# A layer step on one core: the sample tokens' part of a depthwise convolution moved from VectorE to GpSimd

## The chip, the cores and the metric

The kernel runs on one core of a Trainium2 chip. Its time is the device time of one execution in microseconds; a kernel is judged by the median of several executions. The profile shows one execution: TensorE (PE, with its weight loads as PEld), VectorE (DVE), ScalarE (ACT), GpSimd (POOL), and the queues from which SyncE (SP), ACT and POOL issue DMAs. Every engine and every queue works through its own instructions in one fixed order.

## The reference, cut to what matters

One layer of a gated decoder is computed for 1024 prompt tokens and 64 sample tokens (8 sequences of 8) at width 1024. A combined input projection gives a convolution value and gate, q, k and v of three attention groups, and several gates. The attention branch runs dilated windows; the convolution branch is

```python
u = a_val * jax.nn.sigmoid(a_gate)                     # (tokens, 1024 channels)
# prompt: 30 zeros in front; sample: the last 30 values of each sequence in front (state_conv)
u_hist = jnp.concatenate([state_conv, u], axis=1)
conv_raw = depthwise_valid(u_hist, conv_w)             # out[t, c] = sum_j conv_w[j, c] * u_hist[t + j, c], j = 0..30
c = jax.nn.silu(layer_norm(conv_raw + conv_b, conv_ln_g, conv_ln_b))
```

Both branches are gated, projected, merged, projected again and normalised. All arithmetic is in float32. The updated caches are outputs too.

## The kernel before

The 1088 tokens (1024 prompt, then 64 sample) lie along the free axis, channels on the 128 partitions. Every projection tile (128 output channels) is three chunks of 384, 352 and 352 tokens, and each chunk is 24 matmuls: 8 blocks of the inner width, each as three products of a high and a low part (`proj_chunk`, L186). For that ACT makes a high part of each weight tile (`split`, L117) and DVE the low part (L118). Two buffers each hold the raw, high and low weight tiles; the raw tile's load (L130) is on SP's queue.

The order of every engine's instructions is fixed when the program is built: a planner simulates the engines and takes, for each, the instruction that is ready and has the highest priority. `tc.high_priority(LP)` with LP = -800 puts the convolution's arithmetic behind everything else that is ready.

The stages: the loads and the first projections, with V projected for the three groups (to 318 us in the profile); the prompt's attention in 12 units (4 head pairs by 3 groups), between which the q and k projections of the unit two ahead and the convolution's channel tiles 0 to 4 are placed (`B_CONV`); the sample's attention in four pairs `pr` with convolution tiles 5 to 7 (`W_CONV`) and the merge gates; then the LayerNorm over the convolution's channels (reading the results back from a DRAM buffer `cvd`, L771), and the output projections, which are on TensorE alone in the main.

In the prompt's attention a burst of scores S goes through PE (L346), DVE (bias and minimum, L356), ACT (exponent, L363), PE (transposes, L375), DVE and ACT (copies, L383 and L381) and PE (values, L399). `combine` weighs three groups, and its small transfers (L446 `stn`, L473 `wd`, L478 `wb`) and the statistics' stores (L426, L430 `scr`) are issued from POOL. In the sample's attention, POOL copies the queries into a spread-out tile `qf` (L646, 24 copies for a pair) that PE's score matmuls (L655, L663, L667) read.

For channel tile c, `conv_inputs` projects gate and value and leaves u in two tiles: `ub` (30 zeros and 1024 prompt values; two buffers, slots 21 and 22) and `us` (8 sequences of 30 state and 8 new values, 304 columns; three views that lie in the `keep` tiles). The state's columns come by a DMA from SP (L493); the new ones are written last by DVE (L514). POOL stores the convolution states (L515, L516). `conv` then runs 31 taps on DVE, each as one instruction over the prompt's 1024 columns (L526, L529) and one over the 64 sample values (L527, L531), into one tile `cv` (slot 23), which POOL stores into `cvd` (L533). The sample's taps 0 to 22 read state columns alone, so that they can run ahead of the projection; taps 23 to 30 need u.

Of the kernel before, what the change touches and what calls it, by code (L numbers as in the profile page):

```python
# [11 lines left out]
ALU = mybir.AluOpType  # L12
# [4 lines left out]
P = 128  # L17
D = 1024
KT = D // P
NP_ = 1024  # L20
NS = 64
NT = NP_ + NS
# [19 lines left out]
def trunk_kernel(ctx, tc, I, O):  # L42
    nc = tc.nc
    sync, act, dve, pool, pe = nc.sync, nc.scalar, nc.vector, nc.gpsimd, nc.tensor
# [12 lines left out]
    def nm(s):  # L57
        uid[0] += 1
        return f"{s}_{uid[0]}"

    def slot(i, shape, dt=F32, n="s"):
        return sp.tile(shape, dt, tag=f"S{i}", name=nm(n))
# [39 lines left out]
    for q in range(4):  # L102
        w = slice(q * 256, (q + 1) * 256)
# [3 lines left out]
    for q in range(2):  # L107
        w = slice(q * 512, (q + 1) * 512)
# [13 lines left out]
    def cload(name, shape):  # L122
        t = const.tile(shape, F32, name=nm(name))
        sync.dma_start(out=t, in_=I[name])
        return t

    def load_w(src, n, raw=None, parts=1):
        if raw is None:
            raw = wp.tile([P, D], F32, tag="raw", name=nm("raw"))
            sync.dma_start(out=raw[:, :n], in_=src)  # L130
        hi = wp.tile([P, D], F32R, tag="hi", name=nm("hi"))
        lo = wp.tile([P, D], F32R, tag="lo", name=nm("lo"))
        with tc.high_priority(HP):
            for i in range(0, n, n // parts):
                s = split(hi[:, i:i + n // parts], lo[:, i:i + n // parts], raw[:, i:i + n // parts])
            pace(s)
        return hi, lo
# [29 lines left out]
    convw = cload("conv_w", [P, 8, 31])  # L167
    convb = cload("conv_b", [P, 8])
# [47 lines left out]
    keep = [slot(18, [P, NT], n="keep"), None, slot(20, [P, NT], n="keep")]  # L216
# [3 lines left out]
    usv = []  # L220
# [266 lines left out]
    cvd = dram.tile([8, P, NT], F32, name="cvd")  # L487

    def conv_inputs(c):
        ub = slot(21 + c % 2, [P, PAD + NP_], n="ub")  # L490
        us = usv[c % 3]
        pool.memset(ub[:, :PAD], 0.0)
        sync.dma_start(out=us[:, :, :PAD], in_=I["state_conv"][c])  # L493
        wg = load_w(I["w_in"][F_AGATE + c], D)
        wv = load_w(I["w_in"][F_AVAL + c], D)
        b = b_sb[:, F_AVAL + c:F_AVAL + c + 1]
        bg = b_sb[:, F_AGATE + c:F_AGATE + c + 1]

        def spans(c0, cn):

            n = min(cn, NP_ - c0)
            out = [(slice(0, n), ub[:, PAD + c0:PAD + c0 + n], lambda a: a)]
            if n < cn:
                out.append((slice(n, cn), us[:, :, PAD:], lambda a: a.rearrange("p (b t) -> p b t", b=8)))
            return out

        for c0, cn in CHUNKS:
            ps = proj_chunk([(*wg, xhi, xlo)], c0, cn)
            for sl, dst, view in spans(c0, cn):
                act.activation(out=dst, in_=view(ps[:, sl]), func=AF.Sigmoid, bias=bg)  # L510
        for c0, cn in CHUNKS:
            ps = proj_chunk([(*wv, xhi, xlo)], c0, cn)
            for sl, dst, view in spans(c0, cn):
                dve.scalar_tensor_tensor(out=dst, in0=view(ps[:, sl]), scalar=b, in1=dst, op0=ALU.add, op1=ALU.mult)  # L514
        pool.dma_start(out=O["convp"][c], in_=ub[:, NP_:])  # L515
        pool.dma_start(out=O["convs"][c], in_=us[:, :, 8:])  # L516
        return ub, us

    def conv(c, ub, us):
        acc = slot(23, [P, NT], n="cv")  # L520
        accs = acc[:, NP_:].rearrange("p (b t) -> p b t", b=8)
        for j in range(31):
            w = convw[:, c, j:j + 1]
            if j == 0:
                cb = convb[:, c:c + 1]
                dve.tensor_scalar(out=acc[:, :NP_], in0=ub[:, :NP_], scalar1=w, scalar2=cb, op0=ALU.mult, op1=ALU.add)  # L526
                dve.tensor_scalar(out=accs, in0=us[:, :, :8], scalar1=w, scalar2=cb, op0=ALU.mult, op1=ALU.add)  # L527
            else:
                dve.scalar_tensor_tensor(out=acc[:, :NP_], in0=ub[:, j:j + NP_], scalar=w, in1=acc[:, :NP_],  # L529
                                         op0=ALU.mult, op1=ALU.add)  # L530
                dve.scalar_tensor_tensor(out=accs, in0=us[:, :, j:j + 8], scalar=w, in1=accs,  # L531
                                         op0=ALU.mult, op1=ALU.add)
        pool.dma_start(out=cvd[c], in_=acc)  # L533


    snew = dram.tile([3, 8, NS, NS], F32, name="snew")
# [43 lines left out]
    for u, (f, g) in enumerate(units):  # L580
        if g == 0:
            res = []
        q, k = qk.pop(u)
        sample_new_scores(f, g, q, k)
        scr = None if g == 0 else dram.tile([NP_, 4], F32, name=nm("scr"))
        res.append(prompt_attention(f, g, q, k, load_v(f, g), scr))
        if g == 0 and todo:
            combine(*todo.pop())
        if u + 2 < len(units):
            project_qk(u + 2)  # L590
        if u < 2:
            project_v(u + 1)
            if u == 1:
                keep[1] = slot(19, [P, NT], n="keep")
                usv += [keep[i][:, c:c + 304].rearrange("p (b t) -> p b t", b=8)
                        for i, c in ((0, 12 * NS), (1, 0), (1, 304))]
        if u in B_CONV:
            c = B_CONV.index(u)
            cu = conv_inputs(c)
            with tc.high_priority(LP):  # L600
                conv(c, *cu)
        if g == 2:
            attn[f] = slot(14 + f, [P, NT], n="attn")
            todo.append((f, res))
# [143 lines left out]
    def gate(f, dst):  # L748
        pool.dma_start(out=dst, in_=gated(f, AF.Sigmoid, rotate("gst", (3, 4))))
# [3 lines left out]
    for pr in range(4):  # L753
        sc = sample_scores(pr)
        if pr == 0:
            combine(*todo.pop())
            kvs += [9, 10, 11]
            odt += [slot(12 + i, [P, 2, 512], n="od") for i in range(2)]
        for c in W_CONV[pr]:
            u = conv_inputs(c)  # L760
            with tc.high_priority(LP):
                conv(c, *u)
        sample_values(pr, *sc)
        for _ in range(4):
            gate(*gates.pop(0))
    sample_out()
    credit[1] = 1.25
    cv = []
    for c in range(8):
        t = slot(6 + c, [P, NT], n="cv")  # L770
# [76 lines left out]
    for i in range(8):  # L847
        hi, lo = load_w(I["w_b"][i], 512)
        t = slot((0, 1, 2, 3, 16, 17, 4, 5)[i], [P, NT], n="tf")
# [40 lines left out]
    for i, t in enumerate((0, 1, 2, 3, 8, 4, 5, 6, 7)):  # L890
        n = min(P, NT - t * P)
# [14 lines left out]
        for c0, cn in ((0, 512), (512, 256), (768, 256)) if last else ((0, 512), (512, 512)):  # L906
# [8 lines left out]
            for j, (a, b) in enumerate(ops):  # L915
                pe.matmul(ps[:, :cn], a, b, start=(j == 0), stop=(j == len(ops) - 1))  # L916
            dve.scalar_tensor_tensor(out=r[:n, s], in0=xr[:n, s], scalar=ALPHA, in1=ps[:n, :cn],
                                     op0=ALU.mult, op1=ALU.add)
# [12 lines left out]
        for s in parts:  # L931
            dve.scalar_tensor_tensor(out=y[:n, s], in0=r[:n, s], scalar=mv[:n, 0:1], in1=lng[:n, s],
                                     op0=ALU.subtract, op1=ALU.mult)
        dve.reciprocal(out=mv[:n, 4:5], in_=mv[:n, 3:4])
        newton(mv[:n, 4:5], mv[:n, 2:3], mv[:n, 5:6])
        for s in parts:
            dve.scalar_tensor_tensor(out=y[:n, s], in0=y[:n, s], scalar=mv[:n, 4:5], in1=lnb[:n, s],
                                     op0=ALU.mult, op1=ALU.add)
# [136 lines left out]
```

## Time and profile before

| what | value |
|---|---|
| median of 3 runs | 1416.22 us (1413.43, 1416.22, 1421.27) |
| profiled execution, its own time | 1413.38 us |
| its span, first to last instruction | 1411.6 us |
| mean granted TensorE clock | 0.999 |
| busy: PE / PEld / DVE / ACT / POOL | 1394.8 / 1265.8 / 844.0 / 444.7 / 162.9 us |

Busy time is the time in which at least one instruction of an engine is under way. Instructions of PE and of DVE overlap a little with the next one, so that durations are longer than the distance between starts.

### The profile page before, as it was taken

Reading aid. Unit: us, or ns where it says so; the run is one execution under the profiler, and the core shown is the slowest. Engines: PE = TensorE matmul, PEld = TensorE weight load, DVE = VectorE, ACT = ScalarE, POOL = GpSimd, SP = SyncE. Lnnn points to the kernel's source line nnn. Section 1 sums busy time; section 2 is a strip of 40 time slices with the busy share of each in tenths; the row PEclk is TensorE's granted clock in tenths of the full one; section 3 lists DMA queues with packets and bytes.
Section 4 is the critical chain, followed back from the end, with each engine's and each line's share of the span. In section 5 each row is a group of like instructions: output and inputs, shape, how many; then the busy total and the mean of one; then the engine's idle time right before and its main releaser. Section 6 shows DMA issues by size and latency. Waiting matters only on the chain.

```text
span 1411.6 us, 21936 instructions
## 1 busy us (share of the span) xinstructions
PE 1394.8 (99%) x8682; PEld 1265.8 (90%) x8682; DVE 844.0 (60%) x1632; ACT 444.7 (32%) x984; POOL 162.9 (12%) x302
## 2 busy tenths in 40 slices
PE   9999999999999999999999999999999999999997
PEld 8989888899999998999887788898899999999886
DVE  4223131328959779599989785681367425335686
ACT  5204041134434434246531212122246422103220
POOL 2010111110111111102270402000000000000000
PEclk9999999999999999999999999999999999999999
DMA  6629385265855575656488666549653437435321
GB/s 232 215 102 337 117 299 208 87 225 173 249 180 186 197 217 160 219 173 180 138 245 332 244 259 263 165 184 373 223 191 134 162 111 230 142 93 157 120 90 75
DMA packets 85110, 271.27 MB, mean 192 GB/s; under 512 B 20912, under 2 KB 40688, under 8 KB 83600
## 3 DMA queue, kind: packets, MB, share of 16 engines
q1 hardware_dynamic: 70704, 147.16, 31.0%
q10 hardware_dynamic: 2816, 87.30, 17.6%
q0 software_dynamic: 11488, 35.42, 7.6%
q8 instruction: 68, 1.11, 0.3%
q14 instruction: 34, 0.28, 0.1%
HBM read 236.39 MB, written 120.74 MB: 253 GB/s over the span
## 4 chain that ended last, share of the span: by engine, by line
PE 83%; DVE 8%; DMA 3%; issue 3%; ACT 2%; POOL 1%; SPq 0%; DVEq 0%; ACTq 0%; POOLq 0%
PE mm L186 57%; PE mm L284 9%; PE mm L916 7%; DVE cv L529 4%; PE S L346 2%; PE O L399 1%; PE PT L375 1%; ACT P L363 1%; PE O L700 1%; PE S L655 1%; DMA wb<-wd 1%; PE mm L292 1%; DVE lo L118 1%; DVE P L356 1%; PE S L663 1%
## 5 line engine op out<-in xcount | busy, mean ns | idle before, releaser
L186 PE MATMUL mm<-x,hi 128*128 128x352 f32 (+1 forms) x3648 | 912.8, 330 | 1.0 <-ACT x L117 0.6
L186 PEld LDWEIGHTS mm<-x,hi 128*128 128x128 f32 x3648 | 643.3, 188 | 35.0 <-issue 28.9
L186 PE MATMUL mm<-x,lo 128*128 128x352 f32 (+1 forms) x1824 | 600.2, 329 | 0.0
L186 PEld LDWEIGHTS mm<-x,lo 128*128 128x128 f32 x1824 | 342.5, 188 | 12.3 <-issue 10.8
L529 DVE SCALAR_TENSOR_TENSOR cv<-ub,conv_w,cv 128x1024 f32<-128x1024 f32 x240 | 307.1, 1280 | 1.9
L117 ACT ACTIVATE hi<-raw 128x1024 fp32r<-128x1024 f32 (+2 forms) x88 | 86.1, 980 | 272.0 <-PE mm L186 214.2
L118 DVE TENSOR_TENSOR lo<-raw,hi 128x1024 fp32r<-128x1024 f32 (+2 forms) x88 | 98.9, 1125 | 103.5 <-ACT hi L117 91.6
L284 PE MATMUL mm<-vhi,x 128*128 128x512 f32 x384 | 119.1, 390 | 0.0
L363 ACT ACTIVATE P<-P,st 128x128 f32<-128x128 f32 (+1 forms) x192 | 84.2, 440 | 74.7 <-DVE st L356 69.3
L744 ACT ACTIVATE gst<-mm,b_in 128x352 f32<-128x352 f32 (+1 forms) x72 | 40.1, 558 | 150.0 <-PE mm L186 113.8
L284 PEld LDWEIGHTS mm<-vhi,x 128*128 128x128 f32 x384 | 72.1, 188 | 15.0 <-issue 0.2
L285 DVE TENSOR_TENSOR vst<-mm,vb 128x512 f32<-128x512 f32 x24 | 16.6, 692 | 104.8 <-PE mm L284 104.8
L284 PE MATMUL mm<-vlo,x 128*128 128x512 f32 x192 | 74.9, 390 | 0.0
L531 DVE SCALAR_TENSOR_TENSOR cv<-keep,conv_w,cv 128x64 f32<-128x64 f32 x240 | 68.3, 285 | 3.3
L356 DVE CUSTOM_DVE_ANT_0 P<-S,bias 128x128 f32<-128x128 f32 (+1 forms) x192 | 55.0, 347 | 11.1 <-PE S L346 11.1
L916 PE MATMUL mm<-wol,mh 128*128 128x512 f32 (+1 forms) x152 | 57.5, 378 | 0.0
L916 PE MATMUL mm<-woh,mh 128*128 128x512 f32 (+1 forms) x152 | 57.5, 378 | 0.0
L916 PE MATMUL mm<-woh,ml 128*128 128x512 f32 (+1 forms) x136 | 51.3, 377 | 0.0
L646 POOL COPY qf<-keep 64x16 f32<-64x16 f32 x96 | 48.0, 512 | 26.1 <-PE S L655 16.1
L284 PEld LDWEIGHTS mm<-vlo,x 128*128 128x128 f32 x192 | 36.1, 188 | 7.6 <-issue 0.2
L383 DVE COPY PT<-PT 128x512 f32<-128x512 f32 x36 | 24.7, 686 | 28.8 <-PE PT L375 26.3
L346 PE MATMUL S<-qkv,qkv 64*128 64x128 f32 (+1 forms) x384 | 40.3, 339 | 0.0
(187 smaller groups left out, 1291.8 us busy)
## 6 DMA issues: line engine op xcount, KB each, us to landing
out_nb_dram<-in_cache_dram ACTq DMA_DIRECT2D x64, 1020.0 KB
raw<-in_w_in_dram SPq DMA_DIRECT2D x66, 512.0 KB
kv<-in_g3k_dram SPq DMA_DIRECT2D x32, 512.0 KB
kv<-in_g3v_dram SPq DMA_DIRECT2D x32, 512.0 KB
out_nb_dram<-in_cache_dram ACTq DMA_DIRECT2D x16, 1008.0 KB
kv<-in_g2k_dram SPq DMA_DIRECT2D x16, 512.0 KB
kv<-in_g2v_dram SPq DMA_DIRECT2D x16, 512.0 KB
raw<-in_w_v_dram SPq DMA_DIRECT2D x12, 512.0 KB
```

The lines of the kernel that those rows point to most:

```text
L117: h = act.activation(out=dst_hi, in_=src, func=AF.Copy)
L118: dve.tensor_tensor(out=dst_lo, in0=src, in1=dst_hi.bitcast(F32), op=ALU.subtract)
L186: pe.matmul(ps[:, :cn], a, b, start=(i == 0), stop=(i == len(ops) - 1))
L284: pe.matmul(ps, a, b, start=(i == 0), stop=(i == len(ops) - 1))
L346: m = pe.matmul(ps[:, h, off[t]:off[t] + nb * P], q[hs, qc], k[hs, kc], start=True, stop=True)
L356: dve.tensor_tensor_reduce(out=pr[:, h, c], in0=ps[:, h, c], in1=un["bias"][:, h, b0:b0 + nk], scale=-1.0, scalar=3e38, op0=ALU.add, op1=A ...
L363: x["exp"] = act.activation(out=pr[:, h, c], in_=pr[:, h, c], func=AF.Exp, scale=-1.0, bias=st[:, t, h, 0:1], accum_out=st[:, t, h, 1:2])
L529: dve.scalar_tensor_tensor(out=acc[:, :NP_], in0=ub[:, j:j + NP_], scalar=w, in1=acc[:, :NP_], op0=ALU.mult, op1=ALU.add)
L531: dve.scalar_tensor_tensor(out=accs, in0=us[:, :, j:j + 8], scalar=w, in1=accs, op0=ALU.mult, op1=ALU.add)
L646: pool.tensor_copy(out=qfull(g)[hs, f].rearrange("p (r j h) -> p r j h", r=4, j=4)[:, :, :, 2 * f + h2], in_=qs[hs, g * 4 + f, 16 * pr:16 ...
L744: act.activation(out=st[:, c0:c0 + cn], in_=ps, func=func, bias=b_sb[:, f:f + 1])
L916: pe.matmul(ps[:, :cn], a, b, start=(j == 0), stop=(j == len(ops) - 1))
```

## The change

The sample's 31 taps leave `conv`. A new function `conv_sample` does them on GpSimd: one instruction multiplies a sliding view of `us` (six taps, 8 sequences, 8 tokens: 384 products) with six weights that are broadcast over the tokens; four more such products are added to it; the 31st tap is a product of 64. The 384 sums are folded to 192 and then to 64, the last product and the bias are added, and a DMA of its own stores 64 columns. Its two scratch areas lie where the third `us` view was, so that `us` alternates between two.

```diff
-        us = usv[c % 3]
+        us = usv[c % 2]
...
     def conv(c, ub, us):
-        acc = slot(23, [P, NT], n="cv")
-        accs = acc[:, NP_:].rearrange("p (b t) -> p b t", b=8)
+        acc = slot(23, [P, NP_], n="cv")
...
-                dve.tensor_scalar(out=accs, in0=us[:, :, :8], scalar1=w, scalar2=cb, op0=ALU.mult, op1=ALU.add)
...
-                dve.scalar_tensor_tensor(out=accs, in0=us[:, :, j:j + 8], scalar=w, in1=accs,
-                                         op0=ALU.mult, op1=ALU.add)
-        pool.dma_start(out=cvd[c], in_=acc)
+        pool.dma_start(out=cvd[c, :, :NP_], in_=acc)
+
+    def conv_sample(c, us):
+
+        sums, prods = keep[1][:, 304:688], keep[1][:, 688:1072]
+
+        def products(out, j0, jn):
+            win = us[:, :, j0:j0 + 8]
+            part, rest = list(win.ap[0]), [list(x) for x in win.ap[1:]]
+            win = bass.AP(win.tensor, win.offset, [part, [1, jn]] + rest)
+            w = convw[:, c, j0:j0 + jn].unsqueeze(2).unsqueeze(3).to_broadcast([P, jn, 8, 8])
+            pool.tensor_tensor(out=out[:, :64 * jn].rearrange("p (j b t) -> p j b t", b=8, t=8), in0=win, in1=w,
+                               op=ALU.mult)
+
+        def add(n, other):
+            pool.tensor_tensor(out=sums[:, :n], in0=sums[:, :n], in1=other, op=ALU.add)
+
+        products(sums, 0, 6)
+        for j0 in (6, 12, 18, 24):
+            products(prods, j0, 6)
+            add(384, prods)
+        products(prods, 30, 1)
+        add(192, sums[:, 192:])
+        add(64, sums[:, 64:128])
+        add(64, sums[:, 128:192])
+        add(64, prods[:, :64])
+        add(64, convb[:, c:c + 1].to_broadcast([P, 64]))
+        pool.dma_start(out=cvd[c, :, NP_:], in_=sums[:, :64])
...
             with tc.high_priority(LP):
                 conv(c, *cu)
+                conv_sample(c, cu[1])
```

## Rows read from the trace of the kernel before

**Rows 1.** The page: busy time of each engine, and tenths in 40 slices

```profile
PE 1394.8 (99%) x8682; PEld 1265.8 (90%) x8682; DVE 844.0 (60%) x1632; ACT 444.7 (32%) x984; POOL 162.9 (12%) x302
...
PE   9999999999999999999999999999999999999997
...
DVE  4223131328959779599989785681367425335686
```

**Rows 2.** Four stretches: length, then busy us (instructions) of each engine

```profile
317.60:952.80 635.20, 629.84 (x4306) 563.90 (x4304) 512.99 (x972) 226.43 (x543) 116.16 (x208) 1.00 0.63 209
599.90:705.80 105.90, 104.44 (x784) 93.73 (x782) 100.45 (x207) 57.20 (x144) 19.19 (x34) 1.00 0.53 164
...
952.80:1411.60 458.80, 449.28 (x2595) 419.89 (x2591) 236.38 (x429) 129.16 (x232) 2.23 (x5) 1.00 0.47 162
```

**Rows 3.** PE's waits in the whole span: us in total, times, longest

```profile
PE PT L375 <- ACT P L363: 3.1, 2, 1.7
PE S L663 <- POOL qf L646: 1.4, 1, 1.4
PE mm L186 <- DVE lo L118: 1.2, 1, 1.2
```

**Rows 4.** The last of the 40 slices, in the same columns as rows 2

```profile
1376.30:1411.60 35.30, 27.00 (x142) 23.17 (x140) 22.66 (x65) 2.32 (x11) 0.00 (x0) 0.94 0.20 75
```

**Rows 5.** The sample's taps on DVE: min/median/max ns, first and last start

```profile
L531 DVE SCALAR_TENSOR_TENSOR cv<-keep,conv_w,cv x240: 241/283/609, 267.1 to 906.5; 128x64 f32<-128x64 f32 x120
...
L527 DVE TENSOR_SCALAR cv<-keep,conv_w,conv_b x8: 306/314/373, 266.8 to 861.1; 128x64 f32<-128x64 f32 x8
```

**Rows 6.** DVE in order of time, with taps of prompt and sample in turn

```profile
775.57 0.30 DVE L531 SCALAR_TENSOR_TENSOR cv<-keep,conv_w,cv 128x64 f32<-128x64 f32 x1
775.79 1.27 DVE L529 SCALAR_TENSOR_TENSOR cv<-ub,conv_w,cv 128x1024 f32<-128x1024 f32 x1
776.99 0.30 DVE L531 SCALAR_TENSOR_TENSOR cv<-keep,conv_w,cv 128x64 f32<-128x64 f32 x1
777.21 1.27 DVE L529 SCALAR_TENSOR_TENSOR cv<-ub,conv_w,cv 128x1024 f32<-128x1024 f32 x1
```

**Rows 7.** The sample's taps alone: DVE busy us (instructions) in two stretches

```profile
317.60:952.80 635.20, 61.43 (x218) 1.00 0.63 209
599.90:705.80 105.90, 7.00 (x25) 1.00 0.53 164
```

**Rows 8.** POOL's arithmetic: busy us, mean ns, by line

```profile
L85 POOL MEMSET ones<- 128x128 f32 x1 | 0.2, 204 | 0.3 <-POOLq L1065 0.3
...
L172 POOL MEMSET eps<- 128x1 f32 x1 | 0.1, 98 | 0.0
```

**Rows 9.** POOL's query copies and memsets: min/median/max ns, first and last start

```profile
L646 POOL COPY qf<-keep x96: 205/214/1432, 658.9 to 879.1; 64x16 f32<-64x16 f32 x96
...
L613 POOL MEMSET qf<- x1: 527/527/527, 658.4 to 658.4; 128x512 f32 x1
L612 POOL MEMSET qf<- x1: 953/953/953, 708.4 to 708.4; 128x1024 f32 x1
```

**Rows 10.** POOL's copies of 512 columns, the same columns

```profile
L297 POOL COPY keep<-vst x6: 599/606/607, 104.8 to 269.7; 32x512 f32<-32x512 f32 x6
```

**Rows 11.** POOL in order of time, where DVE runs taps (rows 6)

```profile
774.43 4.20 POOL L646 COPY qf<-keep 64x16 f32<-64x16 f32 x3
```

**Rows 12.** POOL in order of time behind channel tile 0, and around the sample's first pair

```profile
322.85 0.87 POOL L516 DMA_DIRECT2D out_convs_dram<-keep  x1 [0.21 <-issue]
...
663.77 0.92 POOL L516 DMA_DIRECT2D out_convs_dram<-keep  x1
671.95 0.73 POOL L426 DMA_DIRECT2D scr<-st  x1 [7.26 <-ACT P L363]
676.53 0.92 POOL L446 DMA_DIRECT2D stn<-scr  x1 [3.85 <-DMA scr<-st]
677.44 0.62 POOL L545 DMA_DIRECT2D snew<-sb  x1
696.86 1.34 POOL L430 DMA_DIRECT2D scr<-st  x2 [18.79 <-ACT P L363]
698.24 2.94 POOL L646 COPY qf<-keep 64x16 f32<-64x16 f32 x4
...
709.37 7.73 POOL L646 COPY qf<-keep 64x16 f32<-64x16 f32 x17
```

**Rows 13.** PE in order of time, at the first pair's second score block

```profile
715.56 0.64 PE L663 MATMUL S<-kv,qf 128*32 128x256 f32 x8 [1.40 <-POOL qf L646]
```

**Rows 14.** SP's queue in order of time, behind channel tile 0

```profile
333.95 0.56 SPq L493 DMA_DIRECT2D keep<-in_state_conv_dram  x1
335.58 1.20 SPq L307 DMA_DIRECT2D vt<-vd  x2
340.84 0.33 SPq L130 DMA_DIRECT2D raw<-in_w_in_dram  x1
```

**Rows 15.** The store into `cvd`: min/median/max ns, first and last start

```profile
L533 POOL DMA_DIRECT2D cvd<-cv x8: 531/564/579, 385.0 to 946.1; - x8
```

More of the change, by code (lines that the diff above doesn't have):

```diff
@@ L524, in conv @@
             if j == 0:
-                cb = convb[:, c:c + 1]
-                dve.tensor_scalar(out=acc[:, :NP_], in0=ub[:, :NP_], scalar1=w, scalar2=cb, op0=ALU.mult, op1=ALU.add)
-                dve.tensor_scalar(out=accs, in0=us[:, :, :8], scalar1=w, scalar2=cb, op0=ALU.mult, op1=ALU.add)
-            else:
-                dve.scalar_tensor_tensor(out=acc[:, :NP_], in0=ub[:, j:j + NP_], scalar=w, in1=acc[:, :NP_],
-                                         op0=ALU.mult, op1=ALU.add)
-                dve.scalar_tensor_tensor(out=accs, in0=us[:, :, j:j + 8], scalar=w, in1=accs,
-                                         op0=ALU.mult, op1=ALU.add)
-        pool.dma_start(out=cvd[c], in_=acc)
+                dve.tensor_scalar(out=acc, in0=ub[:, :NP_], scalar1=w, scalar2=convb[:, c:c + 1], op0=ALU.mult, op1=ALU.add)
+            else:
+                dve.scalar_tensor_tensor(out=acc, in0=ub[:, j:j + NP_], scalar=w, in1=acc, op0=ALU.mult, op1=ALU.add)
+        pool.dma_start(out=cvd[c, :, :NP_], in_=acc)
[21 more added lines that the diff above has]
+        pool.dma_start(out=cvd[c, :, NP_:], in_=sums[:, :64])
     snew = dram.tile([3, 8, NS, NS], F32, name="snew")
@@ L595, in trunk_kernel @@
                 usv += [keep[i][:, c:c + 304].rearrange("p (b t) -> p b t", b=8)
-                        for i, c in ((0, 12 * NS), (1, 0), (1, 304))]
+                        for i, c in ((0, 12 * NS), (1, 0))]
         if u in B_CONV:
@@ L762, in trunk_kernel @@
                 conv(c, *u)
+                conv_sample(c, u[1])
         sample_values(pr, *sc)
```

## Prediction

> **What bounds the kernel now.** I read the page first: PE is busy 1394.8 us of 1411.6, nine tenths in every slice but the last, while DVE stands at 60% and POOL at 12% [rows 1]. A busy PE need not be a PE at its peak, so I went on to its waits. In the whole span the three rows that DVE, ACT or POOL cause come to 5.7 us: 3.1 us for exponents before the transposes, 1.4 us for POOL's query copies, 1.2 us for a low weight part [rows 3]. The stretches say the same from the other side. From 317.6 to 952.8 us, where all the convolution's work lies but a few early sample taps, PE is idle 635.2 - 629.8 = 5.4 us [rows 2]. Behind it PE is idle 458.8 - 449.3 = 9.5 us, of which the last slice, with nothing left to multiply, holds 35.3 - 27.0 = 8.3 us [rows 2, 4]; the change doesn't touch that end. So what a lighter DVE can give back is 5.4 + 1.2 = 6.6 us at the most, and that is 0.47% of the time. A measurement of this kernel tells about 0.5% (7 us) from no change.
>
> The reader is to see that the profile bounds the gain tightly and the loss hardly at all: anything that comes late on DVE or POOL can stop PE.
>
> **What leaves DVE.** 240 taps at 0.283 us and 8 first taps at 0.314 us, 68 + 2.5 = 70 us of records [rows 5]. Where they alternate with the prompt's taps they take less: from the start of a sample tap to the next prompt tap is 0.22 us (775.57 to 775.79, 776.99 to 777.21), since records overlap [rows 6]. The saving therefore lies between 248 x 0.22 = 55 us and 70 us of DVE's time. What it is worth is read where PE waits: the two waits for exponents, 3.1 us, are the ones that end behind DVE work in a stretch filled with taps. I take half of them, -1.6 us (bounds 0 and -6.6).
>
> **What comes to POOL.** Per channel tile: five products of 384, one of 64, four additions of 384, one of 192, four of 64, so nine large, one middle and five small ones, and a second store. The trace shows no instruction of POOL with two inputs, so I bound it. The memsets give the price of one pass: 98 ns for 1 column, 527 for 512, 953 for 1024, about 0.83 ns a column [rows 8, 9]. A copy of 512 columns takes 0.60 us [rows 10], one of 16 takes 0.205 [rows 9]: about 0.2 us and 0.8 ns a column. From below, a two-input instruction costs one pass: 0.1 + 384 x 0.83 = 0.42 us. From above, two reads and a write in turn: 0.2 + 3 x 0.32 = 1.16 us. I take two reads in turn with the write hidden, as in the copy, which is the nearest row: 0.2 + 2 x 0.32 = 0.84 us for 384, 0.52 for 192, 0.31 for 64. A tile is then 9 x 0.84 + 0.52 + 5 x 0.31 = 9.6 us, eight tiles 77 us (38 to 103 by the bounds, with the small ones scaled alike). The extra store is one more issue at 0.56 us a tile [rows 15].
>
> POOL has 635 - 116 = 519 us idle in that stretch [rows 2], so its total hides it. Its order doesn't by itself. A query copy that takes 0.205 us alone takes up to 1.43 us [rows 9], and where DVE runs tap after tap, three such copies fill 4.2 us [rows 11], one for each prompt tap at a distance of 1.42 us [rows 6]. So a POOL instruction that reads SBUF waits for the two-input DVE instruction under way, some 1.2 us more each. With that wait 15 instructions take up to 9.6 + 18 = 28 us, and POOL's total grows by 77 to 220 us, still inside its idle time.
>
> **What is split in time.** Products over taps 0 to 17 read only columns 0 to 24, the loaded state, and can run before u exists, as the first 23 sample taps can now. After u there remain two products and two additions of 384, and six smaller ones: 4 x 0.84 + 0.31 + 0.52 + 4 x 0.31 = 5.4 us of work (7.1 by the upper price), up to 17.4 us with a wait in front of each of the ten.
>
> **Moved and added waits.** (1) With two `us` views, SP loads the state of tile c + 2 instead of c + 3 when tile c's products are read out. Today that load is issued at 333.95, 11 us after POOL has begun to store tile 0's states (322.85) [rows 12, 14], and behind it in SP's queue stand the loads of v and, at 340.84, the next raw weights. On POOL the reads of `us` end after five instructions behind u, about 5 x 2 = 10 us: the same place. I cost it at nothing; what hides it is that the weight load behind it waits until 340.8 us anyway. Were POOL 10 us later there, the weights would come some 4 us later. (2) On POOL's queue, what stands behind a late sample instruction is late too: statistics' stores, combine's loads, query copies, state stores. Only the query copies of the first pair have no slack: PE waits 1.4 us for them [rows 3, 13]; later pairs' copies are made as soon as PE has read the last ones. Tile 4's ten instructions fall just ahead of them. The idle there is 7.3 us before 671.95 and 18.8 us before 696.86, together 26 us [rows 12], against at most 17.4 us. So they fit, with one or two instructions perhaps left over; I take +2.5 us, one and a quarter instructions at 0.84 + 1.2 us (bounds 0 and 17). (3) The split store doubles the issues at 0.56 us [rows 15], and the LayerNorm's reads wait for both; the prompt's one comes last (946.1), so nothing is added.
>
> **The sum.** 1413.4 (the profiled execution) - 1.6 + 2.5 = 1414.3 us. The runs' median stands 1416.2/1413.4 = 1.002 above that execution, so the median to expect is 1417 us. This case alone, PE paced as now and small gains and losses in balance, gives 1411 to 1422.
>
> **The rivals.**
> Slower, by DVE held up (chance 0.16). The trace shows POOL waiting for DVE, and no DVE record that grew: but those copies read 16 columns, and a product reads 768. If DVE's two-input instruction waits in turn until POOL's is done, POOL's time is added to DVE's. The place is 599.9 to 705.8 us: DVE is busy 100.45 of 105.9 us there [rows 2], so it has 5.5 us idle, and losing 25 sample taps frees 25 x 0.22 = 5.5 us more [rows 6, 7]. The later parts of tiles 3 and 4 and the early part of one tile bring 2 x 5.4 + 5 x 0.84 = 15 us, 20 by the upper price: DVE, and with it exponents and low weight parts, is 4 to 9 us behind, and PE with it, 1421 to 1426. It decides from 11 us of POOL work in that stretch. Against it: the order is planned anew, and sample work may move out of the stretch. The Trainium skill ("SBUF — State Buffer", section "Who interferes with whom") states this rule: a VectorE instruction with two SBUF inputs contends with a GpSimd instruction that reads SBUF, and whichever comes second waits for the whole of the other. POOL's 1.43 us agrees with it on POOL's side; no row here shows the DVE side. By that rule the whole 77 us would fall on DVE and the saving of 55 to 70 us would be more than used up; without it, DVE is lighter by all of the saving.
>
> Slower, by POOL's queue (0.11). The planner takes POOL's instructions to be short and puts five or more of tile 4's behind 697 us, ahead of the copies for PE's first pair; each costs 0.84 + 1.2 = 2 us with PE standing, 5 give +10 us, 1426. It decides from about four. For it: POOL's waits for DVE depend on what DVE does at that moment. Against it: the 26 us of idle.
>
> Faster (0.10). All 6.6 us of PE's waits vanish, and the lighter DVE lets the planner put bursts closer: 1408. For it: DVE is at its limit in that stretch. Against it: that needs every wait gone and something beyond the rows.
>
> The change doing nothing it says is no case: the taps leave DVE by construction.
>
> **How the numbers follow.** Likeliest 0.63: no change that can be told, 1417 us. Slower by over 0.5%: 0.16 + 0.11 = 0.27. Faster by over 0.5%: 0.10. The range leaves out most of the faster case and the end of the slower ones: 1409 to 1430.
>
> **What would show it.** Right: PE's busy share stays at 99% and its waits from 317.6 us on stay under 10 us; DVE's total falls by about 70 us to about 774; POOL's rises by 77 to 220 us; the large POOL instructions last 0.84 us alone and about 2 us beside taps. The DVE rival shows as prompt taps above 1.28 us or spaced wider than 1.2 us, and as PE's waits for exponents and low parts between 600 and 710 us. The queue rival shows as one long PE wait for query copies near 715 us. The prediction is wrong if PE's waits change by more than 7 us, or if PE's own order of matmuls is planned so differently that its busy time moves.

## The result, and the profile after

The changed kernel takes 1449.72 us (median of 5 runs, 1447.04 to 1452.44) where the kernel before takes 1416.22 us (5 runs, 1413.43 to 1421.27): ratio 1.0234, 95% interval 1.0206 to 1.0261. It is slower by 33.5 us, and outside the predicted range. The profiled executions lie 2.8 us under the median before and 2.7 us over it after, so their spans differ by a little more than that.

The page of the kernel after: busy time of each engine, tenths in 40 slices, and the granted clock.

```profile
PE 1407.2 (97%) x8682; PEld 1273.0 (88%) x8682; DVE 823.5 (57%) x1384; ACT 447.6 (31%) x986; POOL 301.2 (21%) x430
...
PE   9999999999997999999888999999999999999997
...
DVE  4223141239757579398867777492248615334786
...
PEclk9999999999998999999999999999999999999999
```

The reader is to read this page against [rows 1] by a subtraction. The span is 1450.7 us, 39.1 us longer. PE, with the same 8682 instructions, is idle 1450.7 - 1407.2 = 43.5 us where it was idle 16.8 us: 26.7 us are new waits. The other 12.4 us are PE busy for longer with the same work. Its slices show where: one slice of PE at 7 beside a clock of 8, and three at 8. DVE has lost 248 instructions, but only 20.5 us. POOL has gained 138.3 us.

PE's waits of the kernel after, as in [rows 3]:

```profile
PE PT L375 <- ACT P L363: 16.9, 5, 7.3
PE O L722 <- DMA kv<-in_g3v_dram: 5.4, 2, 4.4
PE S L685 <- POOL qf L668: 3.4, 1, 3.4
PE S L564 <- DVE st L356: 2.4, 3, 1.6
PE mm L186 <- ACT qkv L210: 1.9, 1, 1.9
PE mm L186 <- DVE lo L118: 1.2, 1, 1.2
```

The waits behind exponents have grown from 3.1 to 16.9 us. The query copies, on which the prediction's queue step rested, cost 3.4 us where they cost 1.4. The 5.4 us behind loads of cached values (L722) are not followed up here; with two views alone (e1 below) there is one such wait, of 2.4 us.

The taps on DVE (min/median/max ns, first and last start), and the sample's instructions on POOL by shape (busy us, mean ns of one), kernel after:

```profile
L526 DVE SCALAR_TENSOR_TENSOR cv<-ub,conv_w,cv x240: 1242/1285/2148, 323.8 to 981.8; 128x1024 f32<-128x1024 f32 x120
...
L538 POOL TENSOR_TENSOR keep<-keep,conv_w 128x384 f32<-128x384 f32 x40 | 51.2, 1281 | 20.3 <-DMA cvd<-keep 18.3 <-PE mm L292 0.5
L542 POOL TENSOR_TENSOR keep<-keep 128x384 f32<-128x384 f32 x32 | 49.2, 1539 | 2.1
L542 POOL TENSOR_TENSOR keep<-keep 128x64 f32<-128x64 f32 x24 | 25.1, 1044 | 1.8
```

The median tap is unchanged at 1285 ns, but the longest takes 2148, and the mean of the 240 is 1385 ns against 1280 before: 332.4 us in sum against 307.1. So DVE is held: 49 of the 240 taps take over 1.32 us, and each of these has one of the new POOL instructions beside it. And the POOL instructions are held too: the additions of 384 take 1.54 us in the mean.

**One place, followed through.** POOL, DVE and PE of the kernel after, in order of time, at 440 us (the tap at 444.02 is the last of the four of the row above it, shown again by itself):

```profile
439.00 1.96 POOL L538 TENSOR_TENSOR keep<-keep,conv_w 128x384 f32<-128x384 f32 x1 [5.80 <-DMA cvd<-keep]
441.04 1.87 POOL L542 TENSOR_TENSOR keep<-keep 128x384 f32<-128x384 f32 x1
442.98 1.72 POOL L538 TENSOR_TENSOR keep<-keep,conv_w 128x384 f32<-128x384 f32 x1
444.78 1.87 POOL L542 TENSOR_TENSOR keep<-keep 128x384 f32<-128x384 f32 x1
446.60 1.37 POOL L430 DMA_DIRECT2D scr<-st  x2
456.90 0.93 POOL L446 DMA_DIRECT2D stn<-scr  x1 [8.69 <-DMA scr<-st]
...
438.97 6.81 DVE L526 SCALAR_TENSOR_TENSOR cv<-ub,conv_w,cv 128x1024 f32<-128x1024 f32 x4
444.02 1.76 DVE L526 SCALAR_TENSOR_TENSOR cv<-ub,conv_w,cv 128x1024 f32<-128x1024 f32 x1
448.56 1.25 DVE L526 SCALAR_TENSOR_TENSOR cv<-ub,conv_w,cv 128x1024 f32<-128x1024 f32 x1
460.45 0.17 DVE L456 TENSOR_TENSOR mn<-mn,stn 128x16 f32<-128x16 f32 x1 [10.63 <-DMA stn<-scr]
...
462.87 0.69 PE L186 MATMUL mm<-x,hi 128*128 128x384 f32 x1 [1.95 <-ACT qkv L210]
470.81 1.54 PE L375 MATMUL PT<-ident,P 128*128 128x128 f32 x6 [7.25 <-ACT P L363]
```

The same instructions in the kernel before:

```profile
437.34 1.35 POOL L430 DMA_DIRECT2D scr<-st  x2 [6.01 <-ACT P L363]
444.68 0.91 POOL L446 DMA_DIRECT2D stn<-scr  x1 [5.99 <-issue]
...
447.46 0.18 DVE L456 TENSOR_TENSOR mn<-mn,stn 128x16 f32<-128x16 f32 x1 [2.83 <-DMA stn<-scr]
```

Four POOL instructions of 384 take 7.4 us, and the four taps beside them 6.81 us where four at the median would take 5.1: each side makes the other wait. Behind the POOL instructions stand the statistics' stores. They are issued 9.3 us later than before (446.60 against 437.34), now beside two cache copies that ACT issues at 447.33, and it takes 8.7 us until POOL can go on to the load; the load is 12.2 us later. The four instructions are not the whole of the 9.3 us. Ahead of them POOL stands 5.80 us until its own store of the last tile's sums has been read out, since there is one buffer for sums. The exponents' last record ends at 438.5 us; had POOL gone on at 433.2, some three of the four, at 1.9 us each, would have been done by then (an estimate).

DVE, whose next instruction (L456) is the first to use the loaded statistics, stands 10.6 us, with taps and the next burst's reductions queued behind that instruction. So the exponents are late, and PE stands 7.25 us. The 20 profiles of this case bear that chain out at this place. Where DVE's wait at L456 is 4.0 us or less (12 of them, the kernel before among these), PE has no wait above 0.4 us behind it. Where it is 7.0 to 13.7 us (the change, e2, e7, e8, e10, e12, e15, e18), PE stands 2.7 to 8.2 us.

Around PE's waits its clock is lower; stretches of the kernel after, in the columns of [rows 2]:

```profile
462.90:476.60 13.70, 6.45 (x32) 4.55 (x33) 13.63 (x28) 5.16 (x14) 0.98 (x1) 0.50 0.40 131
660.90:664.30 3.40, 3.37 (x22) 3.04 (x24) 3.35 (x5) 3.28 (x5) 0.90 (x2) 0.50 0.00 1
708.60:715.40 6.80, 5.62 (x40) 4.93 (x40) 4.85 (x6) 5.66 (x12) 0.00 (x0) 0.50 0.33 96
746.20:749.60 3.40, 2.72 (x28) 1.34 (x32) 0.15 (x1) 0.00 (x0) 3.12 (x9) 0.50 0.00 0
787.20:790.60 3.40, 3.40 (x20) 0.65 (x12) 2.89 (x5) 0.00 (x0) 0.00 (x0) 0.50 0.51 177
476.60:490.30 13.70, 13.70 (x95) 12.96 (x95) 9.83 (x23) 5.79 (x19) 0.72 (x2) 1.00 0.29 99
```

For 13.7 us the granted clock is 0.50, the 1.2 GHz level, and then 1.00 again, 2.4 GHz. This stretch begins where the wait of 1.95 us ends, at 462.9, and holds the wait of 7.25 us within it. There are five such stretches, together 30.7 us; the others begin within 1.3 us of the end of a wait of PE (2.91, 4.46, 3.38 and 4.38 us). The kernel before has none until its last slice. PE is busy for 21.6 us in the five; at the other level the same work would take half, so 10.8 us of the 12.4 us that PE is busy for longer are accounted for, by this estimate. Where the rest lies is not shown.

A second place shows what one instruction costs: tile 4's instructions, which the prediction named, in POOL's order of time in the kernel after.

```profile
686.19 0.83 POOL L538 TENSOR_TENSOR keep<-keep,conv_w 128x384 f32<-128x384 f32 x1
687.10 1.88 POOL L542 TENSOR_TENSOR keep<-keep 128x384 f32<-128x384 f32 x1
689.06 0.85 POOL L538 TENSOR_TENSOR keep<-keep,conv_w 128x384 f32<-128x384 f32 x1
689.99 1.01 POOL L542 TENSOR_TENSOR keep<-keep 128x384 f32<-128x384 f32 x1
```

A product takes 0.83 us and an addition 1.01 us when no tap is beside them. With a tap beside them, as at 687.10, it is 1.71 and 1.86 us in the median of the whole run.

### The profile page after: what moved, and what is told of

Same layout as the page of the kernel before. It is cut to its first block, busy times and chain, and to the rows that moved or that the text cites. A ratio compares the mean times of both kernels' runs of the same rounds, so it can differ in the third digit from the quotient of the medians.

```text
span 1450.7 us, 21820 instructions
## 1 busy us (share of the span) xinstructions
PE 1407.2 (97%) x8682; PEld 1273.0 (88%) x8682; DVE 823.5 (57%) x1384; ACT 447.6 (31%) x986; POOL 301.2 (21%) x430
## 4 chain that ended last, share of the span: by engine, by line
PE 46%; DMA 3%; POOL 2%; DVE 2%; ACT 1%; issue 1%; SPq 0%; DVEq 0%; ACTq 0%
PE mm L186 34%; PE mm L939 7%; PE O L722 1%; POOL qf L668 1%; PE S L677 1%; DMA kv<-in_g3v_dram 1%; POOL keep L542 1%; PE O L730 1%; DMA kv<-in_g3k_dram 1%; DMA kv<-in_g2k_dram 0%; PE S L685 0%; PE O L736 0%; DMA cvd<-cv 0%; DVE cv L526 0%; DVE x L118 0%
## 5 line engine op out<-in xcount | busy, mean ns | idle before, releaser
L526 DVE SCALAR_TENSOR_TENSOR cv<-ub,conv_w,cv 128x1024 f32<-128x1024 f32 x240 | 332.4, 1385 | 4.7
L542 POOL TENSOR_TENSOR keep<-keep 128x384 f32<-128x384 f32 (+2 forms) x64 | 84.2, 1316 | 3.9
L538 POOL TENSOR_TENSOR keep<-keep,conv_w 128x384 f32<-128x384 f32 (+1 forms) x48 | 56.2, 1171 | 21.0 <-DMA cvd<-keep 18.3
L375 PE MATMUL PT<-ident,P 128*128 128x128 f32 x280 | 39.3, 286 | 17.0 <-ACT P L363 16.9
L375 PEld LDWEIGHTS PT<-ident,P 128*128 128x128 f32 x280 | 34.0, 147 | 20.4 <-ACT P L363 19.5
```

What stands on the lines that cost most here:

```text
L375: m = pe.transpose(pp[:, i * P:(i + 1) * P], x["pr"][:, h, c:c + P], ident)
L526: dve.scalar_tensor_tensor(out=acc, in0=ub[:, j:j + NP_], scalar=w, in1=acc, op0=ALU.mult, op1=ALU.add)
L538: pool.tensor_tensor(out=out[:, :64 * jn].rearrange("p (j b t) -> p j b t", b=8, t=8), in0=win, in1=w, op=ALU.mult)
L542: pool.tensor_tensor(out=sums[:, :n], in0=sums[:, :n], in1=other, op=ALU.add)
```

## The experiments

Ratios are to the kernel before on the same chip, with 95% intervals. Where GpSimd's arithmetic is replaced (e2, e6, e10, e11, e16), the sample's part of the convolution is left out.

**Which part of the change costs anything.** e1 is the kernel before with two `us` views. e2 is the change without the sample's arithmetic (one memset of 64 columns and the store are left). e5 is the change with `conv_sample` on VectorE.

```diff
e1  -        us = usv[c % 3]
e1  +        us = usv[c % 2]
e2  -        products(sums, 0, 6)
...
e2  +        pool.memset(sums[:, :64], 0.0)
e5  -            pool.tensor_tensor(
e5  +            dve.tensor_tensor(
```

> The kernel before, with two views of us in place of three and nothing else. Theory QUEUE (POOL's sample instructions stand ahead of the statistics' transfers; DVE stands still for them) and theory PORT (POOL's reads make the prompt's taps longer) expect no change, 1412 to 1421 us, since POOL does no sample work here. Theory PLAN (two views, or another order, cost the time by themselves) expects 1430 us or more.

> The changed kernel without the sample's arithmetic: a memset of 64 columns and the small store stand in its place, so the sample's convolution is left out. QUEUE and PORT expect the time of the kernel before or a little less, 1406 to 1418 us, since DVE has lost its 248 sample instructions and POOL has none. PLAN expects it to stay near 1450 us.

> The changed kernel with the sample's fifteen instructions a tile on DVE in place of GpSimd: same products and sums, no POOL arithmetic. PORT and QUEUE both expect it near the kernel before, 1410 to 1426 us. ORDER expects 1430 us or more, if the order that comes of other DVE work is what costs.

Measured: e1 1.0008 (0.9986 to 1.0031), e2 1.0031 (1.0002 to 1.0061), e5 1.0027 (1.0008 to 1.0047). So the views and their later state loads are free, and a lighter DVE gains nothing that shows: in e2 DVE is busy 794.7 us, 49 us less than before, and the time isn't shorter. The loss comes with the arithmetic on GpSimd.

**Occupied queue or reads.** e6 replaces each operation by a memset of twice its columns, e10 by two memsets (161 us in all, where the arithmetic took 146 us in the change), e11 by a copy, with one input instead of two. e9 and e8 are the kernel before with two views, the sample's taps on VectorE, with the memsets and with the arithmetic added on GpSimd (its result goes to a buffer that nobody reads).

```diff
e6  +            pool.memset(keep[1][:, 304:304 + 128 * jn], 0.0)
e10 +            for _ in range(2):
e10 +                pool.memset(keep[1][:, 304:304 + cols], 0.0)     # cols 768 or 550
e11 +            pool.tensor_copy(out=sums[:, :n], in_=other)
e8  -        pool.dma_start(out=cvd[c, :, NP_:], in_=sums[:, :64])
e8  +        pool.dma_start(out=cvx[c], in_=sums[:, :64])
```

> The changed kernel with each of the sample's instructions on GpSimd replaced by a memset of twice the columns (768 for a product or sum of 384), so that POOL writes and doesn't read; the sample's convolution is left out. PE's order is that of the run without sample arithmetic (1424 us), DVE's differs in two rows. PORT (POOL's reads of SBUF and DVE's two-input taps hold each other up) expects 1420 to 1430 us, prompt taps at 1285 ns on average and memsets of 0.74 us beside taps. QUEUE (the sample's instructions merely stand ahead of transfers and query copies in POOL's order) expects 1438 us or more.

> The changed kernel with two memsets in place of each of the sample's instructions on GpSimd (twice 768 columns for the large ones, twice 550 for the others), about 1.4 and 1.0 us and 18.6 us a tile: as long as the arithmetic lasted in the changed kernel (146 us in all, 18.3 us a tile), with no read. The sample's convolution is left out; PE's order is that of the runs with no arithmetic and with short memsets. If what costs is that POOL's instructions become long and hold up what stands behind them on POOL, this run is as slow as the change, 1440 us or more. If what costs is that DVE's taps are held up, it stays near the short memsets, 1418 to 1432 us, with taps at 1285 ns.

> The changed kernel with copies of as many columns in place of GpSimd's products and sums: one SBUF input in place of two, so the sample's convolution is left out in effect. If POOL's reads hold up DVE, the prompt's taps lengthen by less than the 25 us of the change, by about half of it, and the time lies between the memsets and the change, 1428 to 1444 us. If not, it is 1426 us or less.

> As the run with the sample on both engines, but with memsets of twice the columns in place of GpSimd's arithmetic. PE's order is the same as with two views alone. PORT expects 1418 to 1430 us. QUEUE expects it as slow as the run with the arithmetic.

> The kernel before with two views (1422 us beside 1423), which keeps all sample taps on DVE, and with the sample's arithmetic on GpSimd besides, stored into a scratch of its own: the added part of the change without the removed part. PORT expects at least what POOL's arithmetic cost beside the run without it (25 us): 1440 to 1465 us, with prompt taps above 1350 ns on average. QUEUE expects the same time, but with taps at 1285 ns. ORDER (the loss comes of the order that DVE gets when it has fewer taps) expects under 1430 us.

| on GpSimd | sample's taps on VectorE kept | sample's taps removed |
|---|---|---|
| nothing | 1 | e2 1.0031 (1.0002 to 1.0061) |
| memsets | e9 1.0060 (1.0037 to 1.0082) | e6 1.0063 (1.0039 to 1.0087) |
| memsets as long as the arithmetic | not tried | e10 1.0054 (1.0031 to 1.0077) |
| copies | not tried | e11 1.0065 (1.0030 to 1.0099) |
| arithmetic | e8 1.0305 (1.0280 to 1.0329) | the change 1.0234 (1.0206 to 1.0261) |

The prompt's taps in e10, e11 and e8, as above, one row of each kernel:

```profile
L526 DVE SCALAR_TENSOR_TENSOR cv<-ub,conv_w,cv x240: 1242/1285/1290, 323.4 to 956.1; 128x1024 f32<-128x1024 f32 x120
```

```profile
L526 DVE SCALAR_TENSOR_TENSOR cv<-ub,conv_w,cv x240: 1241/1285/1815, 323.2 to 954.6; 128x1024 f32<-128x1024 f32 x120
```

```profile
L529 DVE SCALAR_TENSOR_TENSOR cv<-ub,conv_w,cv x240: 1186/1276/2026, 326.0 to 987.0; 128x1024 f32<-128x1024 f32 x120
```

Memsets of 161 us leave every tap at 1.29 us or less, so they don't touch DVE, and a queue that is occupied for so long costs 0.5%, no more than the short memsets do. Copies hold taps (9.4 us in sum) and cost no more: e11 lies below the 1428 us or more that its expectation gave to held taps, so 9 us of holding alone don't show in the time. The copies are also shorter than the arithmetic (104 us against 146), so the number of inputs and the length aren't told apart by this run. The two-input arithmetic holds taps by 25 us in the change (13.6 us in e8, less than its expectation had) and brings 1.0234 - 1.0063 = 1.7%, 24 us, of the change's 2.3%; with all taps kept it brings 2.4%. So the cause is GpSimd's two-input arithmetic while DVE runs taps.

One rival is left in part: the order of all engines is planned anew for each kernel, and the change's matmuls don't stand in quite the order of e2, e6 and e10, which agree with each other. No run keeps the order and changes the arithmetic alone. Against that rival, the five kernels with the arithmetic on GpSimd and others' work behind it (the change, e3, e7, e8, e12) cost 1.5 to 3.1%, and the eight without it (e1, e2, e4, e5, e6, e9, e10, e11) at most 0.7%.

**At which end: held taps, or late transfers behind GpSimd.** e3 issues the statistics' stores from ScalarE and their loads from SyncE; e4 is the kernel before with the same. e7 puts the sample's instructions behind the statistics' loads (tiles 0 to 3) or a pair's query copies (tiles 4 to 7) on GpSimd. e12 does the arithmetic in pieces of two taps (128 columns, 33 instructions a tile) so that no instruction holds a tap for long.

```diff
e3  -                    pool.dma_start(out=d[b], in_=s2[64 * b:64 * b + 64])
e3  +                    act.dma_start(out=d[b], in_=s2[64 * b:64 * b + 64])
e3  -            pool.dma_start(out=stn[:, g], ...)
e3  +            sync.dma_start(out=stn[:, g], ...)
e7  +            with tc.high_priority(LP), tc.issue_after(behind[0].ins):
e7  +                conv_sample(*waiting.pop(0))
e12 -        for j0 in (6, 12, 18, 24):
e12 -            products(prods, j0, 6)
e12 -            add(384, prods)
e12 +        for j0 in range(2, 30, 2):
e12 +            products(prods, j0, 2)
e12 +            add(128, prods[:, :128])
```

> The changed kernel, with the stores of the statistics on ACT's queue and their loads on SP's, so that they stand behind no sample instruction; the order of PE stays the same but for some thirty lines. QUEUE expects most of the 33 us back, 1418 to 1428 us, DVE's wait for the loaded statistics (row L456) from 32 us to under 16, and the 7.8 us wait of PE near 463 us gone. PORT expects 1442 us or more, with the prompt's taps at 1385 ns in both. PLAN expects no change.

> The kernel before with the stores of the statistics on ACT's queue and their loads on SP's, and nothing else: the control for the same edit on the changed kernel. Expected by all theories within 0.5% of the kernel before; if DVE's wait for the loaded statistics (15 us before) falls, PE's two waits for exponents (3.1 us) may go, 1410 to 1420 us.

> The changed kernel, with the sample's instructions put behind the loads of the statistics (tiles 0 to 3) or behind a pair's query copies (tiles 4 to 7) in POOL's order; no transfer changes its queue. QUEUE expects 1416 to 1430 us and DVE's wait for the statistics at 6 to 16 us. PORT expects 1440 us or more, since all the same POOL reads run beside taps. PLAN makes no forecast, since the order differs.

> The changed kernel, complete, with GpSimd's products and sums in pieces of two taps (128 columns) in place of six (384): 33 instructions a tile in place of 15. In the changed kernel a large instruction that ended beside a prompt tap went with a tap longer by 0.5 us, one of 192 columns by 0.15 us, one of 64 by 0.05 us. If what costs is that taps are held up, DVE's busy time grows by 5 to 15 us in place of 29, and the time is 1424 to 1438 us although POOL's instructions last longer in all than in the changed kernel. If what costs is that POOL's instructions beside taps are longer than the planner took them to be, it is 1450 us or more.

Measured: e3 1.0210 (1.0173 to 1.0247), e4 1.0031 (1.0012 to 1.0051), e7 1.0154 (1.0116 to 1.0192), e12 1.0304 (1.0269 to 1.0338). e3 missed what the queue theory expected: DVE's wait for statistics fell from 32.0 to 17.1 us, and the time hardly. e7 decides nothing: DVE still waits 32.1 us for statistics, and PE has a new wait of 10.1 us for query copies, so the move makes work on GpSimd late in another place; its taps are held by 15 us. e12 missed what the theory of held taps expected: taps are held by 9 us in place of 25, and it is the slowest of the four. PE's waits in e12, and its sample instructions on POOL:

```profile
PE PT L375 <- ACT P L363: 25.4, 6, 7.5
PE S L683 <- POOL qf L666: 4.8, 1, 4.8
```

```profile
L542 POOL TENSOR_TENSOR keep<-keep 128x128 f32<-128x128 f32 x112 | 107.7, 961 | 8.1
L538 POOL TENSOR_TENSOR keep<-keep,conv_w 128x128 f32<-128x128 f32 x120 | 91.1, 759 | 31.6 <-DMA cvd<-keep 23.4 <-PE mm L292 0.5
```

In e12 the sample's work holds POOL for 228 us, since each short piece beside a tap is lengthened; so the lateness on POOL's own queue must cost too. Neither end alone explains both e3 and e12.

**Each end by itself.** The last six runs take everything that others wait for off GpSimd: its statistics, state, key, score and weight transfers go to ScalarE and SyncE, the query copies to ScalarE, the padding to VectorE. What is left of the loss then can't come from what stands behind GpSimd, but for the two ties that e17 and e18 undo. e13 is the change, e14 the kernel before, e15 is e12 and e16 is e6, each with these moves; e17 and e18 are e13 and e15 with two more ties undone.

```diff
all -        pool.dma_start(out=wd.rearrange(...), in_=wt)
all +        act.dma_start(out=wd.rearrange(...), in_=wt)
all -                    pool.tensor_copy(out=qfull(g)[hs, f]..., in_=qs[...]...)
all +                    act.activation(out=qfull(g)[hs, f]..., in_=qs[...]..., func=AF.Copy)
...
e17 -        pool.dma_start(out=cvd[c, :, :NP_], in_=acc)
e17 +        act.dma_start(out=cvd[c, :, :NP_], in_=acc)
e17 -        sync.dma_start(out=us[:, :, :PAD], in_=I["state_conv"][c])
e17 +        pool.dma_start(out=us[:, :, :PAD], in_=I["state_conv"][c])
```

> The changed kernel with everything that others wait for taken off GpSimd: statistics' stores, state stores, key stores, sample score stores and the weights' store are issued by ScalarE, statistics' loads and weight loads by SyncE, the query copies are done by ScalarE, the padding's memset by VectorE. GpSimd keeps the sample's arithmetic and the stores into cvd. LATE (GpSimd's instructions last longer than planned beside taps, and what stands behind them on GpSimd is late): nothing stands behind them any more, so the time falls to that of the memset kernels, 1.003 to 1.009 against the kernel before. HELD (VectorE's taps last longer, 25 us in sum, and everything on VectorE is that much late): the taps' sum stays 20 to 30 us above 307 us and the time stays at 1.017 to 1.026.

> The kernel before with the same moves off GpSimd; a control for the moves themselves. Both theories: within 0.5% of the kernel before (0.996 to 1.006). Were it slower than that, the moves cost time on ScalarE or SyncE by themselves, and e13 is to be read against it.

> The kernel of two-tap pieces (e12, 1.030 with taps held by 12 us only) with the same moves off GpSimd. LATE: 1.003 to 1.010, the whole of its loss came from what stood behind its long GpSimd work. HELD: taps are held by 12 us, half as long as in the change, so 1.010 to 1.016.

> The memset kernel (each GpSimd operation of the sample replaced by a memset of twice its columns; the sample's part of the convolution is left out) with the same moves off GpSimd. Both theories: 1.002 to 1.010, taps at 1285 ns with none above 1.4 us; it is the level that e13 should fall to if LATE holds.

> e13 (all that others wait for taken off GpSimd; 1.0116) with the last two things moved that still tied others to the end of GpSimd's work: the store of the prompt's accumulator, which the next tile's first tap waits for (2.4 us in e13), is issued by ScalarE, and the load of the sample's state, which waits on SyncE for GpSimd's reads, is issued by GpSimd itself. Only the held taps are left. If e13's remaining 0.6% over the memsets of e16 (1.0057) is the held taps, nothing changes: 1.009 to 1.014, taps 20 us or more above 307. If it was these two ties, the time falls to 1.004 to 1.008 with the taps held as much.

> e15 (two-tap pieces, all that others wait for taken off GpSimd; 1.0128 with the taps held by only 8 us) with the same two moves. In e15 a first tap waited 9.9 us for the store of the accumulator behind GpSimd's work. If the two ties cost what is left there, 1.005 to 1.009; if the held taps do, it stays at 1.010 to 1.015.

| on GpSimd | others' work on GpSimd too | GpSimd apart | two more ties undone |
|---|---|---|---|
| nothing, taps on VectorE | 1 | e14 1.0031 (1.0012 to 1.0050) | not tried |
| memsets | e6 1.0063 (1.0039 to 1.0087) | e16 1.0057 (1.0031 to 1.0083) | not tried |
| the change | 1.0234 (1.0206 to 1.0261) | e13 1.0116 (1.0082 to 1.0150) | e17 1.0163 (1.0123 to 1.0204) |
| two-tap pieces | e12 1.0304 (1.0269 to 1.0338) | e15 1.0128 (1.0086 to 1.0170) | e18 1.0114 (1.0074 to 1.0153) |

The prompt's taps in e13, and in e16:

```profile
L526 DVE SCALAR_TENSOR_TENSOR cv<-ub,conv_w,cv x240: 1234/1285/2607, 324.2 to 963.7; 128x1024 f32<-128x1024 f32 x120
```

```profile
L526 DVE SCALAR_TENSOR_TENSOR cv<-ub,conv_w,cv x240: 1243/1285/1289, 324.2 to 958.6; 128x1024 f32<-128x1024 f32 x120
```

Both ends cost. Over its memsets the change loses 1.7% with others' work behind it and 0.6% (e13) to 1.1% (e17) without, although its taps are held as long as ever (24 us in e13 and in e17, against e16). So 0.6 to 1.1%, 9 to 16 us, is work that stood behind GpSimd, and 0.6 to 1.1%, 8 to 15 us, is not. For the two-tap pieces the split is 1.7 to 1.8% behind GpSimd and 0.6 to 0.7% not. Each of these differences of two ratios is uncertain by some 0.4 to 0.6% (an estimate from the intervals in the table): in the change both parts are there, and which of them is the larger isn't shown. e13 itself fell between its two expectations, 1.003 to 1.009 and 1.017 to 1.026. The last two ties cost nothing that shows: neither e17 nor e18 is clearly faster than its neighbour, and e17 lies above its expected 1.009 to 1.014, though not clearly above e13.

That the rest is the held taps fits e13 and is not shown for e15, where taps are held by only 7.4 us. One of e15's waits is of another kind: DVE waits 9.0 us for statistics whose load SyncE issued in time, and PE's wait of 5.4 us follows, in the chain shown above. ScalarE's queue, SyncE's queue, DVE and PE there, in order of time, first of e15, then of e16, which has no such wait of PE:

```profile
445.51 1.24 ACTq L154 DMA_DIRECT2D out_nb_dram<-in_cache_dram  x2
...
445.87 0.38 SPq L446 DMA_DIRECT2D stn<-scr  x1
...
454.47 0.17 DVE L456 TENSOR_TENSOR mn<-mn,stn 128x16 f32<-128x16 f32 x1 [9.04 <-DMA stn<-scr]
...
464.79 1.54 PE L375 MATMUL PT<-ident,P 128*128 128x128 f32 x6 [5.44 <-ACT P L363]
```

```profile
445.81 1.22 ACTq L154 DMA_DIRECT2D out_nb_dram<-in_cache_dram  x2
...
445.68 0.38 SPq L446 DMA_DIRECT2D stn<-scr  x1
...
448.06 0.18 DVE L456 TENSOR_TENSOR mn<-mn,stn 128x16 f32<-128x16 f32 x1 [3.07 <-DMA stn<-scr]
```

In e16 the load goes out 0.1 us ahead of two cache copies of 1 MB each and is there by 448.1; in e15 it goes out 0.4 us behind the first of them, 0.3 us ahead of the second, and takes 8.6 us. So part of what is left in e15 is this place, and such shifts come with every new order. No run moves the copies alone.

## Why the prediction was wrong, point by point

- **What bounds the kernel** was right. The taps' leaving gave back none of the 6.6 us at stake (e2, e5); the prediction had taken 1.6.
- **What leaves DVE**: the records fell by 49.5 us in e6 (844.0 to 794.5), somewhat less than the 55 to 70 expected: 0.20 us an instruction, where 0.22 was the lower bound.
- **The price of a POOL instruction alone** was right: 0.83 us for a product of 384 where 0.84 was taken, 1.01 us for an addition; 1.71 and 1.86 us in the median beside a tap, where about 2 was expected. POOL's growth of 138 us lies in the 77 to 220.
- **The step that failed** is the one behind it: "So a POOL instruction that reads SBUF waits for the two-input DVE instruction under way", and with it the count of who waits. It was read one way. A two-input POOL instruction holds the tap beside it as well: the 45 taps in which one of 384 columns ended took 1.87 us in the median where 1.28 is usual, 49 of 240 taps are longer, 25.3 us in sum. This was the rival "DVE held up", with 0.16. Its mechanism is there, and in its stretch, 599.9 to 705.8 us, taps are held by 5.4 us, the size of the 4 to 9 us that it gave for DVE's lag. But it looked at that stretch alone: the held taps are spread from 324 to 944 us. With GpSimd apart, 8 to 15 us of the time are left (e13, e17 against e16). The Trainium skill ("SBUF — State Buffer", section "Who interferes with whom") has whichever comes second wait for the whole of the other. The direction agrees with these rows, where both sides have longer instructions. The prediction's use of it, that the whole 77 us would fall on DVE, doesn't follow from it, since the wait falls on whichever comes second. Of the 240 taps 157 had no such instruction beside them; the taps took 25.3 us more, and GpSimd's arithmetic 146 us in place of the 77 that were priced for it alone.
- **"Only the query copies of the first pair have no slack"** failed too. POOL's longer instructions, and its wait for its own store, put the statistics' store and load near 440 us 9.3 and 12.2 us later, and DVE waits for these with its taps behind (10.6 us there, where it was 2.8). The sum of DVE's waits at L456 doesn't measure this: it went from 15.2 to 32.0 us, but it is 28.9 us in e10 and 31.3 us in e2 too, with no arithmetic on GpSimd; what counts is where PE follows. What stands behind GpSimd cost 9 to 16 us (e13, e17), and about 25 us with e12's pieces. That the query copies themselves cost 2.0 us more (3.4 against 1.4), where 2.5 were taken, is luck: the same wait of 3.4 us stands in e5, where the sample's arithmetic is on VectorE, and one of 4.0 us in e2, where it is left out.
- **No term held the clock.** Each of PE's five waits of 2.9 us or more goes with a stretch at 1.2 GHz, and those make about 10.8 of the 12.4 us by which PE is busy for longer; the 12.4 us are a third of the loss. It comes on top of the waits and goes with them: in e6, with PE idle 18.0 us, it is busy 1399.1 us.
- **The state's load past SP's queue** was rightly costed at nothing (e1).

What stays open: in the change itself, how the two ends share the 24 us to better than the intervals above (the matmuls' order isn't quite the same in e13, e15 and e16), and how much of the part that remains with GpSimd apart is held taps and how much transfers that meet the cache copies. No kernel here was faster than the kernel before.

## What to carry to other kernels

Before work is put on GpSimd, look at what DVE runs at the same time: in this kernel two-input instructions on both sides held each other, so price each at its time beside the other (in the median 0.83 us became 1.71 us for a product beside a tap, and 1.28 became 1.87 us for a tap in which an instruction of 384 columns ended), on both engines. Then look at what stands behind the new instructions on GpSimd's queue, small transfers above all, and follow who waits for these, and with what queued behind. Where TensorE is the bound and its wait is what comes out last, add the stretch at the lower clock that goes with it.

## What the runs showed of the hardware

- The hold on VectorE's two-input taps goes with GpSimd's reads: memsets of 768 columns leave taps at 1.29 us or less (e10), copies lengthen them to 1.82 us at most and by 9.4 us in sum (e11), two-input instructions to 2.15 us at most and by 25.3 us (the change).
- Smaller pieces don't help: GpSimd's additions of 128 columns take 0.96 us in the mean, of 384 columns 1.54 us, so a third of the work takes well over half of the time; the arithmetic goes from 146 to 228 us (e12).
- TensorE's waits of 1.95 and 7.25 us, close behind each other, went with 13.7 us at a granted clock of 0.50, four of 2.9 to 4.5 us with 3.4 to 6.8 us each (the change).
- A small load that was issued 0.4 us behind the first of two 1 MB copies took some 8.6 us, 0.1 us ahead of both some 2.4 us (e15, e16, load from SyncE). The profiles show the same of GpSimd's loads of the statistics near 297 and 445 us: issued 0.7 to 1.8 us ahead of the two copies they landed in 2.7 to 3.0 us (before, e1, e5, e6, e9, e11, e12), 0.2 to 0.6 us ahead in 6.3 to 6.6 us (nine profiles, before and after among them), behind the first or both in 8.2 to 8.7 us (e7, e11).
